# Rows of the band attention in another order: 3, 1, 4, 2, 5, 0, 6, 7 in place of 0 to 7

## The chip and the metric

The kernel runs on one core of a Trainium2 chip. The metric is the device time of one execution in microseconds, the median of three timed executions. The engines are PE (matmuls), DVE (vector work), ACT (activations), POOL (vector work on a second engine) and SP, whose queue here only issues DMAs.

## What is computed

One layer of a mixer on x of shape 1 x 1024 x 1024. One projection is cut into four head groups, each is gated, and an output projection and a layer norm follow. The change touches group B, a band attention with four heads of 64, in which a chunk of 64 positions sees itself and the eight chunks before it:

```python
def chunk_band_attention(q, k, v, rel_bias):
    ...
    s = jnp.einsum('bcqhd,bckhd->bchqk', qc, kb).astype(jnp.float32) * (dh ** -0.5)
    ...
    s = jnp.where(valid[None, :, None, None, :], s + bias[None, None], -jnp.inf)
    p = softmax_f32(s, v.dtype)
    o = jnp.einsum('bchqk,bckhd->bcqhd', p, vb)
    return o.reshape(bsz, seq, h * dh)

def hybrid_layer(x, mem, ...):
    proj = x @ w_in + b_in
    ...
    yb = chunk_band_attention(heads(bq), heads(bk), heads(bv), b_rel)
    yc = dsa_attention(heads(cq), heads(ck), heads(cv), ...)
    ...
    mixed = jnp.concatenate([ya * jax.nn.silu(a_g), yb * jax.nn.silu(bg),
                             yc * jax.nn.silu(cg), ym * jax.nn.silu(mg)], axis=-1)
    y = mixed @ w_out + b_out
    return layer_norm(DEEPNORM_ALPHA * x + y, ln_g, ln_b)
```

The queries of group B are taken in eight rows of 128. The rows do not depend on each other.

## The kernel before

The whole program is one core's stream of instructions, laid out by helpers that weave attention work with projection work. In the part that matters two stretches follow each other, one for each pair of heads of B. `mixes_of_b(pair)` makes eight items, one for each 128-query row `rb`. Row `rb` sees `n` keys: 128, 256, 384 and 512 for rows 0 to 3, and 640 for rows 4 to 7. `mix_of` gives an item its parts:

- `scores`: PE multiplies queries and keys (`qk` matmuls with 64 rows of weights, three products of high and low halves for each of two heads and each piece of up to 512 columns) into two `qk` banks for each piece. DVE reads them, adds the bias and writes the scores into a tile `sc`, one for each head, and keeps the maximum `mx`. ACT makes `nb` from it and takes the exponential in place. `turned` then lets POOL split the result into a high and a low half (`tensor_scalar`, L545, and `tensor_sub`, L546), and SP transposes both by DMA into a tile `pT`: one DMA for `n` up to 512 (L549), two for 640 (the high half at L551, the rest at L552).
- `values`: PE multiplies `pT` with the value tile in `pv_mm`, two matmuls for each 128 keys and head, into a bank `d["pv"]`, whose tag is "pv" for even rows and "pt" for odd rows. Behind the last, DVE and ACT normalise the row (`o`).
- `close`: PE transposes `o` (a `pt` matmul), DVE gates it (`mix`), and SP stores it.

`parts_behind(items, 2)` sets the order of the parts: at step t come the scores of item t, the first values of item t-2, the close of item t-3 and the other values of item t-2. `weave` goes through these parts and spreads 64 filler steps evenly between them, each of three projection matmuls (`acc`, 128 rows of weights, 512 columns): `weave(parts_behind(mixes_of_b(0), 2), B[1].all(B1_ORDER), RATES[2], pace(3), LAG_T)`, and then pair 1 with fillers from C. A third stream, the search for the top 256 keys of group C, is woven in by `pace`; its passes (`jk` on DVE, `jka` on ACT, and at the end a scan on DVE) fill both engines.

An engine takes its instructions in the order in which a scheduler puts them, so an instruction that waits holds up everything behind it on its engine. The tile `sc` has SB = 4 buffers and `pT` has TB = 4, two rows of two heads each; an item therefore uses the buffers of the item two places ahead of it, and its first score must wait until the transposes of that item have read `sc`. The weight loads for the projections (`raw`) stand on SP's queue among the transposes.

## Time and profile before

| | us |
|---|---|
| median of three runs (lowest, highest) | 674.93 (674.66, 675.70) |
| the profiled run | 675.66 |
| its span, first to last instruction | 673.9 |
| PE busy | 638.5 (95%) |
| DVE, ACT, POOL busy | 479.7, 427.0, 355.4 |
| pair 0, from its first `qk` to pair 1's | 315.79 to 390.70 |
| pair 1, to the first `qk` of group C | 390.70 to 461.97 |

The profile is of one execution. A busy PE in it is not PE at its peak: matmuls overlap, and the distance from the start of one to the start of the next says more than the length of one. The times of a pair are read between the first score matmuls of what follows, since the order of work is the same in both kernels ahead of 315.79 and behind 461.97 us.

### The profile page before, as it was taken

What the parts mean: (1) busy time and instruction counts of PE and PEld (TensorE: products, weight loads), DVE (VectorE), ACT (ScalarE), POOL (GpSimd) and SP (SyncE); (2) the same over time, 40 slices, a digit from 0 to 9 for tenths busy, and PEclk for the clock granted to TensorE, in tenths of its full rate; (3) what the DMA queues carried; (4) which work ended last, traced back from release to release, by engine and by line L of the source; (5) the groups of instructions that cost most, each with busy time, mean ns of one, the idle gap of its engine ahead of it and who ended that gap; (6) DMA issues with size and microseconds to landing.
All of it is one profiled execution on the core that took longest, in us unless ns stands there. A gap on an engine that the chain in (4) does not pass through costs nothing.

```text
span 673.9 us, 11068 instructions
## 1 busy us (share of the span) xinstructions
PE 638.5 (95%) x3698; PEld 484.8 (72%) x3698; DVE 479.7 (71%) x1165; ACT 427.0 (63%) x947; POOL 355.4 (53%) x354
## 2 busy tenths in 40 slices
PE   4889999999999999989899999999999999999995
PEld 3867777767877777767566776677677777778785
DVE  6584254688866898999788778985567559787535
ACT  4665244576799988785888986556456675356210
POOL 3682320306346697483547435993214776557851
PEclk9999999999999999999998999999999999999998
DMA  9783520102134545354439625744001574225111
GB/s 281 237 302 107 162 59 23 40 18 82 60 110 110 132 104 121 72 132 130 96 79 149 132 72 110 126 86 143 31 17 48 177 236 140 75 86 196 63 62 63
DMA packets 121669, 75.30 MB, mean 112 GB/s; under 512 B 58976, under 2 KB 111500, under 8 KB 121612
## 3 DMA queue, kind: packets, MB, share of 16 engines
q1 hardware_dynamic: 121612, 74.59, 41.4%
q8 instruction: 29, 0.48, 0.3%
q14 instruction: 28, 0.23, 0.1%
HBM read 46.44 MB, written 17.64 MB: 95 GB/s over the span
## 4 chain that ended last, share of the span: by engine, by line
PE 51%; DVE 12%; ACT 12%; POOL 10%; issue 7%; DMA 7%; SPq 0%; POOLq 0%; DVEq 0%; ACTq 0%
PE acc L94 36%; PE qk L94 6%; PE pv L94 5%; ACT jka L94 5%; DMA pT<-sc 3%; POOL wblk L208 3%; PE pt L94 3%; DVE jk L94 2%; POOL sc L546 2%; ACT sc L94 1%; DMA raw<-in_w_in 1%; DMA xt<-in_x 1%; DMA hr<-h_dram 1%; POOL rs L134 1%; ACT relu L94 1%
## 5 line engine op out<-in xcount | busy, mean ns | idle before, releaser
L94 PE MATMUL acc<-hTh,wblk 128*128 128x512 f32 (+1 forms) x960 | 316.8, 399 | 4.4 <-ACT vT L94 1.7
L94 PEld LDWEIGHTS acc<-hTh,wblk 128*128 128x128 f32 x960 | 176.8, 188 | 50.3 <-issue 6.7
L94 PE MATMUL acc<-hTl,wblk 128*128 128x512 f32 (+1 forms) x480 | 189.9, 396 | 0.0
L208 POOL TENSOR_TENSOR wblk<-raw,wblk 128x512 fp32r<-128x512 f32 x72 | 99.9, 1392 | 127.9 <-ACT wblk L94 124.8
L94 ACT ACTIVATE jka<-score,cand 128x768 int8<-128x768 f32 (+2 forms) x93 | 96.6, 1038 | 15.7 <-DVE cand L94 15.0
L94 PEld LDWEIGHTS acc<-hTl,wblk 128*128 128x128 f32 x480 | 90.5, 188 | 20.6 <-issue 4.0
L94 PEld LDWEIGHTS <-pT 128*128 128x128 f16 x656 | 46.6, 99 | 32.5 <-issue 18.9
L94 PE MATMUL pv<-v,pT 128*128 128x192 bf16 (+1 forms) x528 | 55.4, 238 | 5.6 <-DMA pT<-sc 5.1
L546 POOL TENSOR_TENSOR sc<-sc 128x512 f16<-128x512 f32 (+4 forms) x48 | 55.9, 1170 | 2.3
L94 ACT ACTIVATE wblk<-raw 128x512 fp32r<-128x512 f32 x72 | 44.6, 627 | 18.6 <-PE acc L94 9.1
L94 DVE SCALAR_TENSOR_TENSOR score<-relu,iw,score 128x384 f32<-128x384 f32 (+5 forms) x42 | 42.7, 1039 | 18.4 <-ACT relu L94 16.5
L94 PE MATMUL acc<-woh,mh 128*128 128x512 f32 (+1 forms) x144 | 55.3, 384 | 0.0
L94 PE MATMUL acc<-wol,mh 128*128 128x512 f32 (+1 forms) x144 | 53.6, 372 | 0.0
L94 PE MATMUL acc<-woh,ml 128*128 128x512 f32 (+1 forms) x144 | 53.5, 373 | 0.0
L545 POOL TENSOR_SCALAR sc<-sc 128x512 f16<-128x512 f32 (+4 forms) x48 | 33.4, 698 | 32.3 <-ACT sc L94 28.8
L94 ACT ACTIVATE relu<-qk 128x384 f32<-128x384 f32 (+2 forms) x80 | 35.5, 533 | 22.5 <-PE qk L94 22.4
L94 ACT ACTIVATE sc<-sc,nb 128x640 f32<-128x640 f32 (+7 forms) x64 | 46.5, 729 | 1.2
L94 ACT ACTIVATE pT<-pt 128x512 f16<-128x512 f32 (+3 forms) x48 | 22.4, 485 | 31.2 <-PE pt L94 30.8
L94 ACT ACTIVATE o<-o,ri 128x64 f32<-128x64 f32 x96 | 28.1, 341 | 17.4 <-DVE o L94 17.3
L94 DVE TENSOR_SCALAR_CACHE_REDUCE jk<-planes,lo 128x384 bf16<-128x384 uint16 (+2 forms) x48 | 35.6, 742 | 1.1
L94 DVE TENSOR_SCALAR_CACHE_REDUCE jk<-planes,cand 128x384 bf16<-128x384 bf16 (+2 forms) x45 | 33.5, 744 | 1.1
L94 DVE TENSOR_REDUCE o<-pv 128x128 f32<-128x384 f32 x48 | 26.4, 549 | 10.2 <-PE pv L94 10.0
(204 smaller groups left out, 1241.2 us busy)
## 6 DMA issues: line engine op xcount, KB each, us to landing
raw<-in_w_in SPq DMA_DIRECT2D x32, 512.0 KB, 3.8
xt<-in_x SPq DMA_DIRECT2D x8, 512.0 KB, 4.7
h_dram<-xt SPq DMA_DIRECT2D x8, 512.0 KB, 5.8
gate<-t SPq DMA_DIRECT2D x16, 256.0 KB, 2.1
rawo<-in_w_out SPq DMA_DIRECT2D x8, 512.0 KB, 3.9
hr<-h_dram SPq DMA_DIRECT2D x8, 512.0 KB, 4.9
out<-hr SPq DMA_DIRECT2D x7, 512.0 KB, 2.6
gate<-gate SPq DMA_DIRECT2D x48, 64.0 KB, 2.0
```

The source lines that it names most:

```text
L94: ins = op(*a, **k)
L134: G.tensor_scalar(tmp, var, EPS, 0.0, ALU.add, ALU.add)
L208: G.tensor_sub(t[:, 1], r, f32(t[:, 0]))
L545: G.tensor_scalar(high, sc[:, :n], 1.0, 0.0, ALU.mult, ALU.add)
L546: G.tensor_sub(rest, sc[:, :n], high)
```

## The change

The rows of B are taken in the order of a new table, `B_ITEMS`, in both pairs, and the bank of the values goes by the item's position (even or odd) instead of by its row number. `place` keeps its default of 0 for the other callers of `mix_of`. The number of instructions on each engine stays what it was.

```diff
--- before.py
+++ after.py
@@ -39,6 +39,7 @@
 
 C0_FIRST, LATE = (0, 1, 6, 7, 5), "17 16 15 14 04 13 03 12 02 11 10"
 HR = 2
+B_ITEMS = 3, 1, 4, 2, 5, 0, 6, 7
 BOOST_Q = 2000
 WH = (0, 0)
 MHB = 2
@@ -703,7 +704,7 @@
 
         return Item(scores, [], [lambda: values(0), lambda: values(1)], close)
 
-    def mix_of(kt, rb, kb0, st, near, far_of, last):
+    def mix_of(kt, rb, kb0, st, near, far_of, last, place=0):
 
         by_dma = kt < 4
         q, k, v3 = st
@@ -750,7 +751,7 @@
 
         def values(odd, c):
             if not odd and not c:
-                d["pv"] = bank(("pv", "pt")[rb % 2 and by_dma], "pv")
+                d["pv"] = bank(("pv", "pt")[place], "pv")
             ph, pl = [part[c:] for part in d["p", odd]] if by_dma else d["p", odd, c]
             for j in range(min(4, nk - c)):
                 pv_mm(d["pv"], odd, ph[j], pl[j], v3[:, kb0 + c + j, odd], c + j == 0, c + j == nk - 1)
@@ -1120,7 +1121,7 @@
 
     def mixes_of_b(pair):
         items = []
-        for rb in range(NB):
+        for i, rb in enumerate(B_ITEMS):
             kb0 = max(0, rb - 4)
             nfar = max(0, (rb + 1 - kb0) * P - 256)
 
@@ -1130,7 +1131,7 @@
                 store_mix(2 + pair, rb, t)
 
             items += mix_of(2 + pair, rb, kb0, B[pair].stacks(), lambda odd: nearB[pair][:, odd, :],
-                            lambda lo, hi, nfar=nfar: farB[:, 384 - nfar + lo:384 - nfar + hi], last)
+                            lambda lo, hi, nfar=nfar: farB[:, 384 - nfar + lo:384 - nfar + hi], last, i % 2)
         return items
 
     weave(parts_behind(mixes_of_b(0), 2), B[1].all(B1_ORDER), RATES[2], pace(3), LAG_T)
```

What moves is shown at three places, each a few rows of PE or DVE in the order in which the engine takes them. A number behind a name is a tile's; `acc` is a filler's matmul, `pT` a transposed tile, L94 and L95 are the same helper's line before and after.

PE in pair 0, where the first values start. Rows that only repeat are left out. Before, row 0's second head (`pT_3650`) and row 1's first (`pT_3701`):

```order
L94 MATMUL acc_3814<-hTl1_118,wblk_3657 128x512
L94 LDWEIGHTS pT_3650
L94 MATMUL pv_3745<-v3_3097,pT_3650 128x192
L94 MATMUL pv_3745<-v3_3097,pT_3650 128x128
L94 MATMUL acc_3814<-hTh1_117,wblk_3657 128x512
L94 MATMUL acc_3934<-hTh0_115,wblk_3926 128x512
L94 MATMUL acc_3934<-hTl0_116,wblk_3926 128x512
L94 MATMUL qk_3875<-kh_3489,qh_2871 128x384
L94 MATMUL acc_3934<-hTh0_115,wblk_3926 128x512 x2
L94 LDWEIGHTS pT_3701
L94 MATMUL pv_3818<-v3_3097,pT_3701 128x192
```

After, row 3's first head (`pT_3647`), scores of row 2 (`qk_3812`, `qk_3813`) and row 3's second head (`pT_3652`); each of its heads has four such pairs of matmuls, of which one stands here:

```order
L95 MATMUL acc_3960<-hTh0_115,wblk_3955 128x512 x2
L95 LDWEIGHTS pT_3647
L95 MATMUL pv_3757<-v3_3097,pT_3647 128x192
L95 MATMUL pv_3757<-v3_3097,pT_3647 128x128
L95 MATMUL qk_3812<-kh_3489,qh_2871 128x384
L95 MATMUL qk_3813<-kh_3489,qh_2871 128x384
L95 MATMUL qk_3812<-kh_3489,ql_2872 128x384
L95 LDWEIGHTS pT_3652
L95 MATMUL pv_3757<-v3_3097,pT_3652 128x192
L95 MATMUL pv_3757<-v3_3097,pT_3652 128x128
L95 MATMUL qk_3813<-kh_3489,ql_2872 128x384
```

The first values are row 3's, four pairs of matmuls for a head instead of one, and no filler stands between the heads.

DVE in pair 0, where an item first uses buffers that a transpose must have read. Before, row 3 (`sc_3785`) behind row 2 (`sc_3715`, `sc_3716`):

```order
L94 TENSOR_SCALAR jk_3588,c_1606<-planes_1519,lo_1608 128x640
L94 RECIPROCAL ri_3843<-rsum_3682 128x2
L94 ISA sc_3715,mx_3717<-qk_3718,farB_128 128x128
L94 ISA mx_3717 128x1
L94 ISA sc_3716,mx_3717<-qk_3719,farB_128 128x128
L94 ISA sc_3715,mx_3717<-qk_3718,nearB_3620,mx_3717 128x256
L94 ISA sc_3716,mx_3717<-qk_3719,nearB_3620,mx_3717 128x256
L94 ISA sc_3785,mx_3787<-qk_3788,farB_128 128x256
L94 TENSOR_TENSOR bit_1605<-c_1606,bar_1536 128x6
```

After, row 4 (`sc_3717`, `sc_3718`), whose buffers are row 3's:

```order
L95 TENSOR_SCALAR jk_3588,c_1606<-planes_1519,lo_1608 128x640
L95 RECIPROCAL ri_3780<-rsum_3626 128x2
L95 ISA sc_3717,mx_3719<-qk_3720,farB_128 128x384
L95 ISA mx_3719 128x1
L95 TENSOR_TENSOR bit_1605<-c_1606,bar_1536 128x6
L95 ISA sc_3717,mx_3719<-qk_3722,nearB_3620,mx_3719 128x256
L95 SCALAR_TENSOR_TENSOR thr_1603<-bit_1605,thr_1603 128x6
L95 SCALAR_TENSOR_TENSOR ql_3663<-acc_3838,bias_77,qh_3662 128x512
L95 TENSOR_SCALAR cand_1604<-thr_1603 128x6
L95 CAST lo_1608<-cand_1604 128x3
L95 TENSOR_SCALAR jk_3676,c_1606<-planes_1519,lo_1608 128x384
L95 ISA sc_3718,mx_3719<-qk_3721,farB_128 128x384
```

The third item's scores have search operations and a projection's `ql` between their heads and behind their first piece.

PE in pair 1, where the scores of row 5 are made. Before, the first of its two pieces (`qk_4898` and `qk_4899`, one tile for each head) among fillers (`acc_4964`):

```order
L94 MATMUL qk_4898<-kh_3932,qh_3660 128x384
L94 MATMUL acc_4964<-hTl1_118,wblk_4853 128x512
L94 MATMUL acc_4964<-hTh1_117,wblk_4853 128x512
L94 MATMUL acc_4964<-hTh1_117,wblk_4856 128x512
L94 MATMUL qk_4899<-kh_3932,qh_3660 128x384
L94 MATMUL qk_4898<-kh_3932,ql_3661 128x384
L94 MATMUL qk_4899<-kh_3932,ql_3661 128x384
L94 MATMUL qk_4898<-kl_3933,qh_3660 128x384
L94 MATMUL qk_4899<-kl_3933,qh_3660 128x384
L94 MATMUL acc_4964<-hTl1_118,wblk_4856 128x512
```

After, both pieces (`qk_4826` and `qk_4827`, `qk_4828` and `qk_4829`) behind the close of row 3 (`pt_4798`):

```order
L95 MATMUL pt_4798<-ident_66,o_4738 128x128
L95 MATMUL qk_4827<-kh_3958,qh_3662 128x384
L95 MATMUL qk_4826<-kh_3958,ql_3663 128x384
L95 MATMUL qk_4827<-kh_3958,ql_3663 128x384
L95 MATMUL qk_4826<-kl_3959,qh_3662 128x384
L95 MATMUL qk_4827<-kl_3959,qh_3662 128x384
L95 MATMUL qk_4828<-kh_3958,qh_3662 128x256
L95 MATMUL qk_4829<-kh_3958,qh_3662 128x256
L95 MATMUL qk_4828<-kh_3958,ql_3663 128x256
L95 MATMUL qk_4829<-kh_3958,ql_3663 128x256
L95 MATMUL qk_4828<-kl_3959,qh_3662 128x256
L95 MATMUL qk_4829<-kl_3959,qh_3662 128x256
```

Eleven of the twelve score matmuls of row 5 follow each other now; before, fillers stood between them at three places, of which the rows show the first two. Over the whole two stretches, the listing of before has fillers interrupted 32 times in pair 0 and 38 times in pair 1, that of after 27 and 25 times.

## Rows read from the trace of the kernel before

**Rows 1.** By stretch: length, busy (instructions) of PE, PEld, DVE, ACT, POOL, clock, DMA.

```profile
316.00:391.00 75.00, 69.72 (x398) 50.55 (x397) 62.11 (x204) 65.68 (x146) 40.61 (x44) 0.98 0.55 106
391.00:462.00 71.00, 69.56 (x402) 49.70 (x401) 58.84 (x154) 45.66 (x103) 50.82 (x45) 1.00 0.55 112
```

**Rows 2.** PE in time (start, length, operation): first scores of pair 0, pair 1, C.

```profile
315.79 0.32 PE L94 MATMUL qk<-kh,qh 64*128 64x128 f32 x1
...
390.70 0.32 PE L94 MATMUL qk<-kh,qh 64*128 64x128 f32 x1
...
461.97 0.33 PE L94 MATMUL qk<-kh,qh 64*128 64x128 f32 x2
```

**Rows 3.** PE in time, pair 0: waits, in brackets with what ended them.

```profile
336.37 0.31 PE L94 MATMUL pv<-v,pT 128*128 128x192 bf16 x2 [1.43 <-DMA pT<-sc]
...
358.82 0.26 PE L94 MATMUL pv<-v,pT 128*128 128x192 bf16 x1 [0.92 <-DMA pT<-sc]
...
360.79 0.33 PE L94 MATMUL pv<-v,pT 128*128 128x128 bf16 x2 [0.67 <-DMA pT<-sc]
```

**Rows 4.** Table by stretch: the low clock behind those waits.

```profile
361.00:364.40 3.40, 3.40 (x26) 2.94 (x23) 2.81 (x12) 2.89 (x8) 1.84 (x3) 0.50 0.67 128
```

**Rows 5.** PE in time: a score matmul between fillers, and scores in a group.

```profile
316.61 0.39 PE L94 MATMUL acc<-hTh,wblk 128*128 128x512 f32 x1
316.92 0.38 PE L94 MATMUL qk<-kh,qh 64*128 64x256 f32 x1
317.24 0.50 PE L94 MATMUL acc<-hTh,wblk 128*128 128x512 f32 x1
317.57 0.39 PE L94 MATMUL acc<-hTl,wblk 128*128 128x512 f32 x1
317.80 0.40 PE L94 MATMUL acc<-hTh,wblk 128*128 128x512 f32 x1
...
440.21 0.28 PE L94 MATMUL qk<-kh,ql 64*128 64x256 f32 x2
440.33 0.28 PE L94 MATMUL qk<-kl,qh 64*128 64x256 f32 x2
```

**Rows 6.** PE in time: two value matmuls between fillers.

```profile
455.83 0.31 PE L94 MATMUL pv<-v,pT 128*128 128x192 bf16 x2
455.95 0.48 PE L94 MATMUL acc<-hTh,wblk 128*128 128x512 f32 x1
456.27 0.40 PE L94 MATMUL acc<-hTl,wblk 128*128 128x512 f32 x1
```

**Rows 7.** DVE, ACT, POOL in time at pair 0's start; the transposes' landing, 318 to 392.

```profile
325.77 0.28 DVE L94 CUSTOM_DVE_ANT_0 sc<-qk,nearB 128x128 f32<-128x128 f32 x1
...
336.48 0.42 DVE L94 CUSTOM_DVE_ANT_0 sc<-qk,farB 128x256 f32<-128x256 f32 x1 [1.63 <-DMA pT<-sc]
...
339.87 0.71 ACT L94 ACTIVATE sc<-sc,nb 128x512 f32<-128x512 f32 x1
...
341.47 1.16 POOL L546 TENSOR_TENSOR sc<-sc 128x512 f16<-128x512 f32 x1
...
DMA to landing us min/median/max: 2.3/2.7/5.1
```

**Rows 8.** All engines in time: the fifth row of pair 1, scores to values.

```profile
419.90 0.48 DVE L94 CUSTOM_DVE_ANT_0 sc<-qk,nearB,mx 128x256 f32<-128x256 f32 x1
...
420.65 0.74 DVE L94 SCALAR_TENSOR_TENSOR ql<-acc,bias,qh 128x512 fp32r<-128x512 f32 x1
...
421.62 0.82 ACT L94 ACTIVATE sc<-sc,nb 128x640 f32<-128x640 f32 x1
...
426.28 3.13 POOL L546 TENSOR_TENSOR sc<-sc 128x640 f16<-128x640 f32 x1
...
429.44 1.21 SPq L552 DMA_TRANSPOSE pT<-sc  x1
...
432.89 0.23 PE L94 MATMUL pv<-v,pT 128*128 128x128 bf16 x1 [1.07 <-DMA pT<-sc]
```

## The prediction

> **What bounds the kernel now.** I read the table by stretch first. Before 315.79 us and after 461.97 us the order of work is the same in both kernels, so only the two pairs of band heads can change: pair 0 from 315.79 to 390.70 us (74.91 us) and pair 1 from there to 461.97 us (71.27 us) [rows 2]. In both, PE is busy 93 and 98% of the time, DVE 83% [rows 1], so the end of a pair is PE's work plus PE's waits. Second, the waits: PE idles 5.28 us in the first stretch and 1.44 us in the second [rows 1], and most of it is `pv` matmuls waiting for a transposed probability tile `pT` to land: 1.43, 0.92 and 0.67 us in pair 0 [rows 3] and 1.07 in pair 1 [rows 8]. Third, the clock: TensorE is granted 0.50, its 1.2 GHz level, from 361.0 to 364.4 us, right after the stretch in which PE waited twice for row 4's `pT`; PE was busy all of those 3.40 us, so the fall costs at most half of it, 1.7 us [rows 4]. Everything else of the two pairs is PE's own pace: 74.91 - 5.28 - 1.7 = 67.9 us and 71.27 - 1.44 = 69.8 us.
>
> **Part one: the pace of PE, and what an interruption costs.** PE fills the time between attention pieces with projection matmuls (`acc`), 192 in each pair. The listings of both kernels show how often that run is interrupted: 32 times in pair 0 and 38 in pair 1 before, 27 and 25 after. Of these, interruptions that hold score matmuls (`qk`) number 13 and 18 before, 12 and 14 after; the others (`pv`, and small transposes) 19 and 20 before, 15 and 11 after.
> The price of one with `qk`: from the `acc` at 316.61 to the one at 317.80 us, 1.19 us pass in which three `acc` start; their own pitch is 0.23 (317.57 to 317.80), so 0.50 is left for one `qk` of 256 columns, which inside a group takes 0.12 at most (440.21 to 440.33). The interruption itself costs 0.38 [rows 5]. The price of one without `qk`: two `pv` start at 455.83, the next `acc` at 455.95, and its follower comes 0.32 later instead of 0.23: 0.09 [rows 6].
> These two prices can be tested on the kernel before: pair 1 has five more interruptions with `qk` and one more without, which makes 5 x 0.38 + 0.09 = 2.0 us, and its pace is 69.8 - 67.9 = 1.9 us slower. So I trust them. Pair 0 then gains 0.38 + 4 x 0.09 = 0.74, pair 1 gains 4 x 0.38 + 9 x 0.09 = 2.33, together 3.07 us. The bounds are 1.9 (the five with `qk` alone) and 3.9 (a quarter more).
> The Trainium skill (TensorEngine Tiling (Array Packing), "Key Properties") says that changing the tiling mode drains TensorE. `qk` is 64-row work and `acc` and `pv` are 128-row work, so by that rule a `pv` between `acc` would cost nothing, and the sum would be the five alone, 1.9 us, with a time of 674.5 us. The 0.09 behind a `pv` speaks against taking the rule for the whole cost.
>
> **Part two: the start of pair 0.** Row 3 (512 keys) now comes first instead of row 0 (128). DVE starts its scores where row 0's started, at 325.77, and row 1's pieces stand between its heads, so row 3's scores, six pieces of at most 0.48 with these, are done by about 328.4. ACT runs a search pass and two exponentials of 0.71, POOL a `tensor_scalar` and a `tensor_sub` of 1.16 for each head (the second head's `tensor_sub` now stands behind row 1's two `tensor_scalar`), and a transpose lands 2.3 to 5.1 us after its issue, here about 3 [rows 7]: the two heads land at about 335.3 and 338.1. PE, which has more filler ahead of its first `pv`, arrives at about 335.3: no wait for the first head, 1.7 for the second, about 0.5 for row 1's. Row 4 uses row 3's `sc` and `pT` buffers, and its first score on DVE waits for row 3's transpose, as row 3's did for row 1's before, 1.63 us [rows 7]; here that stall is about 3 us, and the search operations behind it on DVE wait too. Row 4 then lands at about 348.4 and 350.9, PE comes at 347.1: waits of 1.3 and 1.3. The weight load that stood directly ahead of row 4's transposes on SP's queue stands ahead of row 5's now, where PE has slack of 1 us or more; row 5 to row 7: 0.2. Sum 5.0 against 5.28: -0.28. Each landing is an estimate good to 1.2 us, so the sum may be 3 to 8.
> The clock I leave as it is: PE is again kept waiting twice, one wait close behind the other, now near 348 us instead of 359. It can go to -1.7 (no fall) or +1.7 (a second one).
>
> **Part three: pair 1.** PE's only long wait before is for row 4, the fifth row, at 432.89 us (1.07 us). Its way: last score piece at 419.90, exponential of the second head at 421.62, `tensor_sub` on POOL at 426.28, which takes 3.13 us while DVE runs the search's scan, transpose at 429.44 [rows 8]. Now the fifth row is row 5, also 640 wide, and POOL's order around it is the same (sub, scalar, weight block, sub). Ahead of it DVE has scored rows 3, 1, 4, 2 instead of 0 to 3: one 640-wide row in place of a 128-wide one, two heads of 2 x 0.48 - 0.28 = 0.68, and a projection's low part `ql` of 0.74 (420.65) that stood behind [rows 7, 8]: 2.1 us later. It lands at 432.9 + 2.1 = 435.0, less what PE's gain in pair 0 passes on to DVE; I take 434.3. PE arrived at 431.8 before. Now ten more `acc` stand ahead of it (+2.3), seven interruptions fewer (4 x 0.38 + 3 x 0.09 = -1.8), four `pv` fewer (-0.3), and pair 0 ended 1.0 earlier: 431.0. The wait is 3.3 instead of 1.44 for the whole pair: +1.9, with bounds of 0 (POOL's `tensor_sub` misses the scan) and 5 (a weight load on SP delays the landing as well). Rows 6 and 7 stand 17 and 20 us behind it on PE and land in time. The changed bank of `pv` costs nothing: positions alternate between the same two banks as rows did.
>
> **Sum.** -3.07 - 0.28 + 1.9 = -1.45 against the profiled run of 675.66: 674.2. That run is 0.73 above the median of 674.93, so the forecast is 673.5 us. What can be told from no change is 0.2%, 1.35 us; the forecast lies just beyond it.
>
> **The rivals.**
> Rival A, faster: the clock does not fall, because PE's waits for row 4 (1.3 + 1.3 now, 0.92 + 0.67 before [rows 3]) come where it has been busy longer or are met by the landing. That takes 1.7 off: 671.8 us. For it: the mean clock of the first stretch, 0.98, leaves room for the one fall only [rows 1], so the wait of 1.43 at 336.37 brought none. Against: the new ones lie as close together as the old. Chance 0.18.
> Rival B, no change: PE gets ahead of a chain that does not get faster. The interruptions saved are in pair 1, 1.8 of them ahead of the wait for row 5, and every one saved there is waited for if the landing stands; and the landing may be a microsecond later. Then the 3.07 is spent: 674.9 us. For it: DVE is in order and full of search. Against: six interruptions and ten `acc` are saved behind the wait as well. Chance 0.24.
> Rival C, slower: one set of buffers carries rows 3, 4, 5 and 6, all the wide ones, so each wide row's first score stands behind the transposes of the one before. If row 3's second transpose lands one issue later (1.3 us) and row 5's in pair 1 meets the weight load (5.1 instead of 2.7 us to landing [rows 7]), DVE's stalls pass on to rows 4 and 5 and PE pays 1.3 + 2.4 on top of the waits above: 673.5 + 3.7 = 677.2 us. It decides when row 4's second head lands after 352 or row 5's in pair 1 after 437. For it: DVE stalled 1.63 behind a narrower row already. Against: the same buffers come round only every 18 us or so (two of eight rows of 75 us), and a wide row needs about 10 from its scores to the landing. Chance 0.25.
> The forecast itself, 672.3 to 674.7 with its own error: 0.33.
>
> **How the numbers follow.** Faster by over 0.2% (below 673.6): 0.20 of the forecast's 0.33, all of A, 0.05 of B: 0.43. Slower (above 676.3): 0.24 of C and 0.03 of B: 0.27. Same: 0.30. For 8 in 10 the range takes in A's centre and its better half by 0.8, and C's centre: 671.0 to 677.3 us.
>
> **What will show it.** The interruptions: pair 1 without its waits should take about 67.5 us, pair 0 without waits and clock about 67.2. The starts: `pv` waits for row 3's second head near 338 and for row 4's near 348 and 350 us, and one of about 3 us near 434. DVE should show a stall of about 3 us on `pT` near 332 to 335. The forecast is wrong if the waits of pair 0 pass 7 us, if that of pair 1 passes 5, or if the pace does not follow the count of interruptions.

## The result

| | median us (lowest, highest) | profiled run | its span |
|---|---|---|---|
| before | 674.79 (674.33, 675.70) | 675.66 | 673.9 |
| after | 682.75 (681.69, 683.67) | 683.67 | 681.9 |

The changed kernel is slower: ratio 1.0117, interval 1.0102 to 1.0131. The forecast was 673.5, the range 671.0 to 677.3. So the sign is wrong, and the time lies 5.4 us outside the range.

The table by stretch of the changed kernel, cut at the first score matmuls as [rows 2] were: length, busy (instructions) of PE, PEld, DVE, ACT, POOL, granted clock, share and GB/s of DMA. First pair 0 and pair 1, then the four places where the clock falls:

```profile
315.80:390.74 74.94, 70.41 (x398) 51.63 (x397) 59.38 (x193) 61.24 (x140) 40.46 (x44) 0.95 0.51 106
390.74:466.83 76.09, 70.04 (x401) 52.35 (x401) 64.91 (x165) 49.09 (x108) 47.64 (x45) 0.96 0.46 105
338.00:346.00 8.00, 6.64 (x29) 4.89 (x30) 7.20 (x30) 6.55 (x16) 2.39 (x3) 0.58 0.35 84
424.00:428.00 4.00, 3.19 (x12) 2.39 (x13) 3.91 (x17) 1.42 (x3) 1.28 (x1) 0.58 0.69 158
440.00:446.00 6.00, 4.73 (x19) 3.22 (x21) 4.72 (x11) 2.16 (x5) 1.75 (x3) 0.72 0.36 79
638.00:644.00 6.00, 5.19 (x17) 3.98 (x18) 4.79 (x9) 3.17 (x11) 5.40 (x5) 0.72 0.44 160
```

Pair 0 takes what it took (74.94 against 74.91 us [rows 2]), pair 1 takes 76.09 instead of 71.27, and what follows, the last part, whose order of work is unchanged, takes 681.9 - 466.83 = 215.07 instead of 211.93. Length less busy PE is PE's idle time: 4.53 us in pair 0 and 6.05 in pair 1, where [rows 1] gave 5.28 and 1.44.

A mean clock of 0.58 over 8 us is 0.42 / 0.50 x 8 = 6.7 us at the 1.2 GHz level, and half of that, 3.4, is the most it can cost. The falls of pair 1 are 3.4 us each at that level and cost at most 1.7 each. Before there was one such fall, of 3.4 us, in both pairs together [rows 4].

PE in time, the waits over 0.3 us in the two pairs (start, length, operation, and in brackets the wait and what ended it), which answer to [rows 3] and to the last of [rows 8]:

```profile
337.92 0.26 PE L95 MATMUL pv<-v,pT 128*128 128x192 bf16 x1 [1.19 <-DMA pT<-sc]
340.56 1.22 PE L95 MATMUL pv<-v,pT 128*128 128x192 bf16 x8 [1.36 <-DVE mx L95]
367.23 0.38 PE L95 MATMUL qk<-kh,qh 64*128 64x256 f32 x1 [1.06 <-DVE mx L95]
381.85 0.26 PE L95 MATMUL pv<-v,pT 128*128 128x192 bf16 x1 [0.91 <-DMA pT<-sc]
424.81 0.45 PE L95 MATMUL pt<-ident,o 128*128 128x128 f32 x1 [2.97 <-DVE mix L95]
437.71 0.30 PE L95 MATMUL pt<-ident,o 128*128 128x128 f32 x1 [0.76 <-DVE mix L95]
441.27 0.96 PE L95 MATMUL pv<-v,pT 128*128 128x128 bf16 x9 [2.32 <-DMA pT<-sc]
```

Two of them, 1.36 and 1.06 us, end when DVE has read a score bank. The kernel before has such a wait too, which the rows ahead of the prediction leave out:

```profile
353.63 0.44 PE L94 MATMUL qk<-kh,qh 64*128 64x384 f32 x1 [0.86 <-DVE mx L94]
```

The longest is of a kind that the prediction did not have: the `pt` matmul of a `close` waits at 424.81 for a `mix`. A `mix` is DVE's gating of the row closed before, and it reads that row's transpose out of a "pt" bank. There are three "pt" banks in turn, and the second head's score pieces and the values of odd positions also take them, so the close of the second row needs the bank that the gating of the first still holds.

Where was DVE? Its rows ahead of that gating (the search's end and a projection's `ql`; accumulator reads and the other rows between them left out):

```profile
415.19 0.62 DVE L95 SCALAR_TENSOR_TENSOR thr<-bit,thr 128x6 uint32<-128x6 uint32 x1
...
416.21 1.12 DVE L95 TENSOR_TENSOR thr<-thr,hi 128x3 uint32<-128x3 uint32 x1
...
419.01 1.35 DVE L95 SCALAR_TENSOR_TENSOR cand<-thr 128x3 f32<-128x3 f32 x1
420.40 1.01 DVE L95 TENSOR_SCALAR_CACHE_REDUCE jk<-score,cand 128x768 bf16<-128x768 f32 x1
...
421.45 1.15 DVE L95 TENSOR_SCALAR_CACHE_REDUCE jk<-score,cand 128x896 bf16<-128x896 f32 x1
...
422.52 0.75 DVE L95 SCALAR_TENSOR_TENSOR ql<-acc,bias,qh 128x512 fp32r<-128x512 f32 x1
423.19 1.27 DVE L95 TENSOR_SCALAR_CACHE_REDUCE jk<-score,cand 128x1024 bf16<-128x1024 f32 x1
...
424.38 0.28 DVE L95 TENSOR_TENSOR mix<-pt,gate 128x128 f32<-128x128 f32 x1
```

and the same in the kernel before:

```profile
412.09 0.15 DVE L94 SCALAR_TENSOR_TENSOR thr<-bit,thr 128x6 uint32<-128x6 uint32 x1
...
412.82 0.15 DVE L94 TENSOR_TENSOR thr<-thr,hi 128x3 uint32<-128x3 uint32 x1
...
413.49 0.62 DVE L94 SCALAR_TENSOR_TENSOR cand<-thr 128x3 f32<-128x3 f32 x1
414.14 1.01 DVE L94 TENSOR_SCALAR_CACHE_REDUCE jk<-score,cand 128x768 bf16<-128x768 f32 x1
...
415.08 0.28 DVE L94 TENSOR_TENSOR mix<-pt,gate 128x128 f32<-128x128 f32 x1
```

Before, the gating stands behind one of three counting passes and runs at 415.08; after, it stands behind all three and a `ql`, at 424.38, 4.8 us behind the transpose it reads (`pt` at 419.60). PE wanted the bank at 424.81 - 2.97 = 421.84. In a small way the wait was there before: PE stood still for the same gating, for one third of a microsecond.

```profile
415.42 0.38 PE L94 MATMUL qk<-kh,qh 64*128 64x256 f32 x1 [0.35 <-DVE mix L94]
```

The fifth row of pair 1, row 5 now (DVE's last score piece, POOL's second `tensor_sub`, the second head's transpose on SP's queue), answers to [rows 8]:

```profile
427.41 0.48 DVE L95 CUSTOM_DVE_ANT_0 sc<-qk,nearB,mx 128x256 f32<-128x256 f32 x1
```

```profile
436.38 2.26 POOL L547 TENSOR_TENSOR sc<-sc 128x640 f16<-128x640 f32 x1
```

```profile
438.66 1.20 SPq L553 DMA_TRANSPOSE pT<-sc  x1
```

Its scores are ready 7.5 us later than row 4's were (419.90), PE starts on its `pT` at 441.27 instead of 432.89, and waits 2.32 us for it. DVE's search had fallen behind on the way: a pass whose result (`bit`) DVE took at 381.62 us before was taken at 388.67 after. But most of these 7 us were made up again. The result of the search's last pass, before and after:

```profile
410.84 0.92 DVE L94 TENSOR_TENSOR bit<-c,bar 128x6 uint32<-128x6 f32 x1
```

```profile
414.31 0.16 DVE L95 TENSOR_TENSOR bit<-c,bar 128x6 uint32<-128x6 f32 x1
```

It ends at 411.76 before and at 414.47 after, 2.7 us later. So of the 9.3 us by which the gating is later, 2.7 are the search's lag. Another 3.6 lie between that result and the first counting pass (2.4 us before, 5.9 after), and 3.0 are the order: two more counting passes and a `ql` ahead of the gating.

### The profile page after: what moved, and what is told of

Read it like the earlier page. It is cut to its first block, busy times and chain, and to the rows that moved or that the text cites. A ratio compares the mean times of both kernels' runs of the same rounds, so it can differ in the third digit from the quotient of the medians.

```text
span 681.9 us, 11075 instructions
## 1 busy us (share of the span) xinstructions
PE 640.4 (94%) x3698; PEld 489.2 (72%) x3698; DVE 486.2 (71%) x1165; ACT 425.6 (62%) x947; POOL 351.6 (52%) x354
## 4 chain that ended last, share of the span: by engine, by line
PE 36%; DVE 5%; POOL 3%; DMA 3%; issue 3%; ACT 1%; SPq 0%; POOLq 0%; DVEq 0%; ACTq 0%
PE acc L95 25%; PE qk L95 4%; PE pv L95 4%; PE pt L95 2%; DMA pT<-sc 2%; DVE sc L95 1%; DMA hr<-h_dram 1%; POOL hr L1244 1%; DVE hr L95 1%; DVE jk L95 1%; POOL sc L546 1%; POOL hr L1243 1%; POOL sc L547 0%; DVE thr L95 0%; ACT jka L95 0%
## 5 line engine op out<-in xcount | busy, mean ns | idle before, releaser
L95 PE MATMUL acc<-hTh,wblk 128*128 128x512 f32 (+1 forms) x960 | 316.2, 401 | 4.4 <-ACT vT L95 1.7
L95 PEld LDWEIGHTS acc<-hTh,wblk 128*128 128x128 f32 x960 | 178.6, 190 | 51.5 <-issue 6.8
L95 PE MATMUL acc<-hTl,wblk 128*128 128x512 f32 (+1 forms) x480 | 190.8, 398 | 0.0
L95 ACT ACTIVATE jka<-score,cand 128x768 int8<-128x768 f32 (+2 forms) x93 | 96.5, 1038 | 21.7 <-DVE cand L95 20.9
L95 PEld LDWEIGHTS acc<-hTl,wblk 128*128 128x128 f32 x480 | 91.5, 191 | 20.8 <-issue 3.1
L95 PEld LDWEIGHTS <-pT 128*128 128x128 f16 x656 | 46.7, 99 | 32.0 <-issue 17.6
L95 PE MATMUL pv<-v,pT 128*128 128x192 bf16 (+1 forms) x528 | 53.5, 237 | 7.9 <-DMA pT<-sc 4.4
L547 POOL TENSOR_TENSOR sc<-sc 128x512 f16<-128x512 f32 (+4 forms) x48 | 58.5, 1228 | 1.8
L95 ACT ACTIVATE wblk<-raw 128x512 fp32r<-128x512 f32 x72 | 44.5, 627 | 20.6 <-PE acc L95 11.4
L546 POOL TENSOR_SCALAR sc<-sc 128x512 f16<-128x512 f32 (+4 forms) x48 | 30.4, 641 | 50.9 <-ACT sc L95 50.8
L95 DVE SCALAR_TENSOR_TENSOR score<-relu,iw,score 128x384 f32<-128x384 f32 (+5 forms) x42 | 42.8, 1040 | 18.4 <-ACT relu L95 16.4
L95 PE MATMUL acc<-woh,mh 128*128 128x512 f32 (+1 forms) x144 | 55.8, 388 | 0.0
L95 PE MATMUL acc<-woh,ml 128*128 128x512 f32 (+1 forms) x144 | 54.2, 378 | 0.0
L95 PE MATMUL acc<-wol,mh 128*128 128x512 f32 (+1 forms) x144 | 54.2, 376 | 0.0
L95 ACT ACTIVATE relu<-qk 128x384 f32<-128x384 f32 (+2 forms) x80 | 35.5, 532 | 22.5 <-PE qk L95 22.4
L95 ACT ACTIVATE sc<-sc,nb 128x640 f32<-128x640 f32 (+7 forms) x64 | 46.4, 728 | 0.8
L95 ACT ACTIVATE pT<-pt 128x512 f16<-128x512 f32 (+3 forms) x48 | 22.4, 485 | 31.1 <-PE pt L95 30.9
L95 DVE TENSOR_SCALAR_CACHE_REDUCE jk<-planes,lo 128x384 bf16<-128x384 uint16 (+2 forms) x48 | 35.7, 743 | 1.0
L95 ACT ACTIVATE o<-o,ri 128x64 f32<-128x64 f32 x96 | 27.9, 340 | 11.1 <-DVE o L95 10.9
L95 DVE TENSOR_REDUCE o<-pv 128x128 f32<-128x384 f32 x48 | 26.4, 549 | 11.4 <-PE pv L95 11.3
L95 DVE TENSOR_SCALAR_CACHE_REDUCE jk<-planes,cand 128x384 bf16<-128x384 bf16 (+2 forms) x45 | 33.5, 744 | 1.1
```

The source lines that it names most:

```text
L95: ins = op(*a, **k)
L546: G.tensor_scalar(high, sc[:, :n], 1.0, 0.0, ALU.mult, ALU.add)
L547: G.tensor_sub(rest, sc[:, :n], high)
```

## Experiments

In the tables, waits are length less busy PE. All ratios are against runs of the kernel before on the same chip; the intervals are 95%.

**The same two kernels again.** Both unchanged.

> The changed kernel once more, for its last part: there its profile loses 3.2 us in the output stage, whose instructions are in the same order in both kernels: a wait of 1.8 us on TensorE near 638 us and a fall of the clock behind it, after a load of hr from memory landed later. If that belongs to the change (the output stage reached 4.8 us later meets something at a fixed time), every profile of it shows the wait. If it is chance, this profile shows none, and the time is 680 us.

> The kernel before once more, for a second profile of it on this chip: how far its pairs, its waits and its last part differ from execution to execution. If the wait near 633 to 639 us in the output stage (0.66 to 1.81 us in every kernel with a new order so far) belongs to these kernels, it is absent here, as in the first profile; if it is chance, it may stand here too. Pair 0 74.9, pair 1 71.3, last part 211.9 us if nothing varies.

| | ratio (interval) | pair 0 | pair 1 | waits | last part |
|---|---|---|---|---|---|
| after | 1.0117 (1.0102, 1.0131) | 74.94 | 76.09 | 4.53 + 6.05 | 215.07 |
| after again | 1.0108 (1.0089, 1.0128) | 73.85 | 76.73 | 3.10 + 4.95 | 212.74 |
| before | 1 | 74.91 | 71.27 | 5.28 + 1.44 | 211.93 |
| before again | 0.9995 (0.9973, 1.0017) | 73.45 | 71.62 | 5.43 + 1.98 | 212.0 |

What comes back each time is pair 1: 76.1 and 76.7 against 71.3 and 71.6, with a wait of 2.97 and 2.89 for the gating. Pair 1 of the second profile:

```profile
391.23:467.96 76.73, 71.78 (x401) 53.48 (x400) 65.60 (x166) 50.15 (x111) 48.30 (x46) 0.93 0.46 104
```

Its waits are 1.1 us less than the first time and it still takes longer: a mean clock of 0.93 is some 10 us at the 1.2 GHz level, which can cost 5 us. The longer last part does not come back (212.74), so most of its 3.1 us was this one execution's; the second one lost 1.6 us to a clock fall near 52 us instead, far ahead of the change. In the kernel before, the clock fall near 361 did not come back.

**Each half alone.** The new order and the new bank rule in pair 0 only, and in pair 1 only:

```diff
-        for i, rb in enumerate(B_ITEMS):
+        for i, rb in enumerate(B_ITEMS if pair == 0 else range(NB)):
```

```diff
-        for i, rb in enumerate(B_ITEMS):
+        for i, rb in enumerate(B_ITEMS if pair == 1 else range(NB)):
```

> The new order in pair 0, the old one in pair 1. Theory 'lag': in pair 0 VectorE stalls for transposes (3.3 us at 335.5 and 2.2 us at 362.6 in the changed kernel), the search queued behind those stalls falls one pass, 5 to 7 us, behind and stays so, and pair 1 starts with VectorE late whatever its own order: pair 0 takes 74.9 us as in the changed kernel, pair 1 has TensorE waits of 3 to 6 us instead of 1.4 and one or two falls of the clock, 677 to 680 us in all. Rival 'own order': what pair 1 loses comes from its own rows in the order 3, 1, 4, 2; then this run has pair 0 at 74.9, pair 1 at 70 to 71.5 and 674 to 676 us.

> The old order in pair 0, the new one in pair 1. 'Lag': VectorE comes to pair 1 on time, its first score near 392 to 395 us instead of 397.8, the fifth row's scores end near 423 instead of 427.8, TensorE waits for it about 3 us, one fall of the clock: 674 to 677 us. 'Own order': TensorE waits 6 us and more in pair 1, two falls of the clock, 679 to 682 us.

| | ratio (interval) | pair 0 | pair 1 | waits | both pairs |
|---|---|---|---|---|---|
| pair 0 only | 1.0018 (0.9999, 1.0038) | 74.54 | 70.01 | 3.67 + 2.80 | 144.55 |
| pair 1 only | 1.0014 (0.9997, 1.0032) | 75.21 | 71.58 | 5.75 + 2.33 | 146.79 |

Neither half loses more than 0.2%, and neither interval excludes no loss at all: the pairs take 144.6 and 146.8 us against 146.2 before and 151.0 with both. (The 144.6 leave out nine `pv` of pair 1, which stand behind the first score matmul of C there; twelve `pv` in a group take 1.0 us before, so this is some 0.7 us.) With pair 0 only, 676.80 us lies between the two forecasts. So it is neither pair 1's own row order nor the lag that pair 0 hands on, each by itself. In both halves the gating of pair 1's first row runs earlier than after the whole change, at 417.5 and 419.9, and nobody waits long for it.

**Rows 2 and 4 exchanged.**

```diff
-B_ITEMS = 3, 1, 4, 2, 5, 0, 6, 7
+B_ITEMS = 3, 1, 2, 4, 5, 0, 6, 7
```

> The order 3, 1, 2, 4, 5, 0, 6, 7 in both pairs: rows 2 and 4 change places, so that row 4 uses the buffers of row 1 (256 keys) and the third item is 384 wide and not 640; fillers are interrupted 19 and 26 times (27 and 24 in the changed kernel by the same count, 32 and 37 before). If wide rows one behind the other in one set of buffers hold VectorE, this gives most of the loss back: VectorE's stall at the third item stays (it still waits for row 3) but the search is less late, TensorE waits under 5 us in all and no more than two falls of the clock, 671 to 676 us. If the loss is the late start of the first values (row 3 being first) or the mere presence of a wide row early, it stays at 679 to 683 us.

Ratio 1.0031 (1.0016, 1.0047); pairs 74.21 and 72.32 with waits of 5.67 and 3.57 us. The first gating of pair 1 runs at 418.57, behind two of the counting passes. Exchanging two neighbours moves the gating by 6 us and removes most of the loss; the time, 677.59 us, lies between the two ranges that I had set.

**Without the search in the pairs.** The search's passes are not woven into the two pairs but come later, in the kernel before and in the changed one. It then lies open elsewhere, so the total says nothing; the pairs do.

```diff
-PACE = ((10,), (8,), (9,), (10,), (15,))
+PACE = ((10,), (8,), (9,), (0,), (0,))
```

> The kernel before with no search woven into the two pairs (its paces there are 0; the search then runs behind pair 1, so the whole time is longer and only the two pairs are compared). Theory 'both together': the loss of the changed kernel needs the search being late on VectorE and the new order in pair 1. Without the search VectorE has slack: TensorE waits under 3 us in the two pairs here, pair 0 about 70 to 73 us and pair 1 about 69 to 70.

> The changed kernel, likewise without the search in the two pairs. 'Both together': the new order then loses nothing in pair 1, its fillers are interrupted less often, and its two pairs take as long as those of the kernel before without the search or up to 3 us less, with no wait of more than 2 us in pair 1. Rival: the wide rows in one set of buffers hold the chain by themselves, search or not: then this pair of kernels differs by 4 to 5 us as the originals do.

The changed kernel without it, pair 0 and pair 1:

```profile
314.94:386.19 71.25, 67.52 (x397) 49.85 (x396) 36.27 (x120) 39.53 (x96) 40.16 (x44) 1.00 0.51 111
386.19:453.71 67.52, 67.52 (x403) 49.55 (x402) 28.39 (x97) 35.37 (x85) 39.47 (x43) 1.00 0.55 118
```

The pairs take 138.77 us with the new order and 72.16 + 67.80 = 139.96 with the old one (totals 715.4 and 718.7). PE has no wait in pair 1 in either, and the new order loses nothing: the loss needs the search on DVE beside it. The 1.2 us that the order gains are no more than two profiles of one program differ by (146.18 and 145.07 for the kernel before).

**The new order with the old bank rule.**

```diff
-                            lambda lo, hi, nfar=nfar: farB[:, 384 - nfar + lo:384 - nfar + hi], last, i % 2)
+                            lambda lo, hi, nfar=nfar: farB[:, 384 - nfar + lo:384 - nfar + hi], last, rb % 2)
```

> The new order with the bank of the values by row number, as it was, instead of by position. Rows 3 and 1, 4 and 2, and 0 and 6 then follow each other in the same bank. If the second half of the change does what it is for, rows 1, 2 and 6 wait for the normalisation of the row ahead, about 1 us on TensorE for each of the three in each pair: up to 6 us slower than the changed kernel, 683 to 688 us. If the alternation costs nothing, 682 to 683 us as the changed kernel.

> The row order 3, 1, 4, 2, 5, 0, 6, 7 with the value banks by row number, once more and with more rounds, to see whether it is faster than the kernel before. By its first profile the pairs take 143.2 us against 146.2 before (and 145.1 and 144.9 in the two later looks at kernels with the old order), with two clock falls in it. Theory that the order of rows is worth its pace (interruptions 14 and 13 with scores, 7 and 4 without, against 13, 18, 19, 20) when no counting pass stands ahead of a gating: 0.996 to 0.999 of the kernel before, 672.5 to 674.5. Rival, that the clock falls take all of it in most executions: 0.999 to 1.002.

First 0.9978 (0.9955, 1.0002), then, with more runs, 0.9981 (0.9960, 1.0002). The pairs of the first:

```profile
316.18:387.44 71.26, 68.26 (x388) 51.47 (x388) 58.92 (x195) 62.04 (x141) 38.54 (x43) 0.98 0.50 102
387.44:459.40 71.96, 68.19 (x390) 51.42 (x390) 59.85 (x157) 45.63 (x102) 48.35 (x46) 0.98 0.51 115
```

The whole loss is gone. The 143.2 us for both pairs make the gain look larger than it is, since 19 `pv` of the last rows stand behind the first score matmul of C in this kernel, some 1.6 us; the medians have it at 0.2%, within their intervals. I had expected the old rule to leave the time as it was or to make it worse by putting neighbours into one bank. What happened is that the scheduler, given another bank for four of the eight rows of each pair (3, 2, 5 and 0), laid out everything else anew: interruptions 14 and 13 with `qk`, 7 and 4 without, and a search one pass further at most rows. The gating still comes late, at 423.01, but PE's next `pt` matmul stands at 423.43 and finds it done.

**Shorter counting passes.** The changed kernel with the three last counting passes of the search over 128 columns each instead of 768, 896 and 1024; so part of the counting is left out.

```diff
-            n = (RBS[i] + 1) * P
-            V.tensor_scalar(junk()[:, :n], score[RBS[i]], f32(cand[:, i:i + 1]), None, ALU.is_ge,
+            n = P
+            V.tensor_scalar(junk()[:, :n], score[RBS[i]][:, :n], f32(cand[:, i:i + 1]), None, ALU.is_ge,
```

> The changed kernel with one thing cut: the three counting passes of the search on DVE (768, 896 and 1024 columns, once in the program) look at 128 columns each, so part of the counting is left out. Row order, banks and the order of PE's work ahead of the passes stay. In the changed kernel the gating (mix) of pair 1's first row stood on DVE behind these passes, 1.01 + 1.15 + 1.27 us plus a projection's low part of 0.75, and PE waited 2.97 us for it at 424.81. Theory that this queue holds PE's next transpose: the wait falls by about the 2.5 us taken out, to under 0.8, the clock does not fall near 425, and pair 1 takes 71.5 to 73.5 us instead of 76.1; total 677.5 to 680.5. Rival, that the bank is held by something else (the values of an odd position, which share its ring): the wait stays over 2 us and pair 1 over 75 us, total 681 to 683. Rival, that the late search alone costs (PE then pays at row 5's landing instead): wait near 425 gone, but over 4 us at row 5's values, pair 1 over 75.

Ratio 1.0198 (1.0165, 1.0230); pairs 74.12 and 74.92. The wait did not fall to under 0.8 us; it stayed, which is what the rival on the bank had said. The rows, DVE and then PE:

```profile
424.18 1.15 DVE L95 TENSOR_SCALAR_CACHE_REDUCE jk<-score,vth 128x896 bf16<-128x896 f32 x1
...
425.25 0.29 DVE L95 TENSOR_TENSOR mix<-pt,gate 128x128 f32<-128x128 f32 x1
```

```profile
425.68 0.30 PE L95 MATMUL pt<-ident,o 128*128 128x128 f32 x1 [2.95 <-DVE mix L95]
```

The scheduler put the time into the next step of the search: a pass of the masks (`vth`) now stands ahead of the gating. So the edit did not isolate what it was meant to: the gating is late again, behind other work of the search, and PE's wait ends with it again. Whether it is the search ahead of the gating at all was left to the next experiment. (The last part, whose order changed as well, took 6.7 us more than after the change: score matmuls there waited up to 2.59 us for DVE, and the clock was at its 1.2 GHz level from 570.0 to 576.9.)

**The end of the search held back.** Every instruction stays. Five empty steps ahead of the three counting passes, with the pace raised to match, make the search's end come later. In the changed kernel and, as a control, in the kernel before:

```diff
-PACE = ((10,), (8,), (9,), (10,), (15,))
+PACE = ((10,), (8,), (9,), (10,), (20,))
...
+        for _ in range(5):
+            yield
         for i in range(NV, NR):
             n = (RBS[i] + 1) * P
             V.tensor_scalar(junk()[:, :n], score[RBS[i]], f32(cand[:, i:i + 1]), None, ALU.is_ge,
```

> The changed kernel, complete, with five empty steps in the search ahead of its three last counting passes, so that they come later. On DVE all is in the same order up to the two normalising operations of pair 1's first row, but then the gating (mix) of that row comes ahead of the counting passes instead of behind them. Theory that this queue on DVE holds PE's next transpose: the wait of 2.97 us near 425 is under 0.8 us, the clock does not fall there, pair 1 takes 71 to 73 us instead of 76.1 and 76.7; total 676.5 to 680. Rival, that the bank or the row order makes the wait: over 2 us again near 425, total 681 to 684. Rival, that PE pays the time at row 5's values instead: wait near 425 gone, over 4 us near 437 to 442, total 680 to 684.

> Control: the kernel before with the same five empty steps. There the gating of pair 1's first row stood between the counting passes and PE did not wait for it. Theory: nothing to gain, 0.998 to 1.003 of the kernel before, pair 1 71 to 72.5 us. Rival, that moving the end of the search later helps by itself: under 0.997.

The changed kernel with it, 676.91 us, ratio 1.0015 (0.9998, 1.0033). Pair 0 and pair 1; DVE at the gating; PE there:

```profile
317.41:391.52 74.11, 70.53 (x397) 51.83 (x396) 58.73 (x192) 60.40 (x137) 39.79 (x44) 0.95 0.51 107
391.52:464.12 72.60, 67.83 (x401) 50.28 (x401) 66.20 (x163) 47.77 (x108) 46.68 (x46) 1.00 0.55 110
```

```profile
421.70 0.73 DVE L95 SCALAR_TENSOR_TENSOR ql<-acc,bias,qh 128x512 fp32r<-128x512 f32 x1
422.35 0.28 DVE L95 TENSOR_TENSOR mix<-pt,gate 128x128 f32<-128x128 f32 x1
...
425.77 1.01 DVE L95 TENSOR_SCALAR_CACHE_REDUCE jk<-score,cand 128x768 bf16<-128x768 f32 x1
```

```profile
423.16 0.30 PE L95 MATMUL pt<-ident,o 128*128 128x128 f32 x1
...
427.71 0.59 PE L95 MATMUL pv<-v,pT 128*128 128x192 bf16 x6 [1.97 <-DMA pT<-sc]
```

The gating comes ahead of the passes, PE does not wait for it, and the clock stays at 1.00 through pair 1: 72.60 us instead of 76.09 and 76.73. This run decides on the search's place: by the ratios (1.0117 and 1.0108 without the hold) 6.3 to 6.9 of the 7.3 to 7.9 us are gone, and in the profiles 3.5 to 4.1 of them in pair 1. It speaks against the bank as the cause, since the bank rule is the changed kernel's. Of the idle time little went (6.05 and 4.95 to 4.77), since PE now waits 1.97 us for a transpose and, at 459.79, 1.33 for another. The gain is clock, the 3.4 us and more that the falls of pair 1 could cost, while the pace is 1.2 us worse. PE's order further on in pair 1 changed with the hold as well, so the gain is the hold's. That the one wait for the gating made the loss is not isolated by it.

The kernel before with it: 672.35 us, ratio 0.9972 (0.9953, 0.9991), the only version here that is faster than the kernel before by its interval:

```profile
315.82:389.42 73.60, 68.04 (x398) 49.18 (x397) 60.65 (x203) 65.22 (x145) 40.72 (x44) 1.00 0.56 108
389.42:458.80 69.38, 69.21 (x402) 49.53 (x402) 61.70 (x154) 45.05 (x103) 49.66 (x45) 1.00 0.54 115
```

I had expected nothing to gain there, and had overlooked PE's 0.35 us for the gating (0.45 in the second profile). Pair 1's idle time goes from 1.44 and 1.98 to 0.17 us, among it the wait for row 4 [rows 8]. So the hold gives 0.3% without the new order too, and not all that it gives the changed kernel belongs to the change. With the search's end held back the old order is the better one: 0.9972 against 1.0015, with intervals that do not meet.

**Other orders and the hold.** Banks by row with another order; two orders, one for each pair, without and with the hold; and banks by row with the hold:

```diff
-B_ITEMS = 3, 1, 4, 2, 5, 0, 6, 7
+B_ITEMS = 1, 7, 0, 4, 3, 5, 6, 2
```

```diff
-        for i, rb in enumerate(B_ITEMS):
+        for i, rb in enumerate(((3, 1, 2, 4, 5, 0, 6, 7),(0, 1, 2, 3, 4, 5, 6, 7))[pair]):
```

> Another order, 1, 7, 0, 4, 3, 5, 6, 2, with the banks by row number. The listing has 13 and 13 interruptions with scores and 11 and 7 without (before 13, 18, 19, 20), and the search on DVE is as far as in the kernel with the banks by row (29, 30, 31, 31 passes ahead of pair 1's first four rows, against 28, 29, 29, 30 in the changed kernel). Theory that pace follows interruptions and the rest follows how far the search is: pace of pairs together 137.7 - 6.0 x 0.38 x 5/6 (5 fewer with scores, 1.9) - 21 x 0.09 (1.9) = 133.9 us, waits and clock falls as in the kernel before (6.7 + 1.7): pairs 142 to 145, total 671 to 675. Rival, that a row order with a wide row 7 second and a narrow one last makes DVE and the landings late whatever the search does: pairs over 147, total over 677.

> Pair 0 in the order 3, 1, 2, 4, 5, 0, 6, 7 and pair 1 in the old order 0 to 7, banks by position. The listing has the search at 28, 28, 28, 29 passes ahead of pair 1's first four rows, a pass later than in the changed kernel (28, 29, 29, 30) and two later than before (29, 29, 29, 30 at the same places or later). Interruptions 10 and 17 with scores, 9 and 20 without. Theory that a late search costs only where wide rows come first in the next pair: pair 1 71 to 73 us, total 673 to 677. Rival, that lateness of the search alone costs: pair 1 over 74.5, total over 679.

> The new row order with banks by row number and the same five empty steps. No wait for a gating was there to remove. Theory: as without them, 0.996 to 1.000 of the kernel before, 672 to 674.5 us. Rival, that the end of the search behind the gating also spares this kernel's 1.97 us wait for row 5's transpose near 441 and the clock fall behind it: pair 1 under 70 us, 669 to 671.5 us.

> Pair 0 in the order 3, 1, 2, 4, 5, 0, 6, 7, pair 1 in the old order, with the same five empty steps. Without them there was no wait for a gating over 0.49 us. Theory: unchanged within 0.3%, 673 to 676 us, pair 1 70.5 to 72 us. Rival, that a later end of the search meets the scores of C: last part over 214 us, total over 676.5.

| | ratio (interval) | pair 0 | pair 1 | waits |
|---|---|---|---|---|
| order 1, 7, 0, 4, ... | 1.0109 (1.0076, 1.0142) | 71.62 | 73.39 | 3.64 + 3.20 |
| two orders | 0.9995 (0.9975, 1.0016) | 73.67 | 71.00 | 5.50 + 1.54 |
| banks by row, held | 1.0010 (0.9993, 1.0027) | 71.81 | 72.94 | 2.57 + 4.15 |
| two orders, held | 0.9991 (0.9977, 1.0005) | 74.68 | 70.61 | 5.87 + 1.39 |

The first took 145.0 us for the pairs, the upper end of what I had set, and 683.25 us in all instead of 671 to 675: it lost its 1.1% in the last part, which took 220.1 us. Its order there is another one too, score matmuls wait 1.69 and 1.72 us for DVE, and the clock is at its 1.2 GHz level from 562.5 to 569.3. Nor was its pace as counted: without waits and clock the pairs take 145.0 - 6.84 - 1.7 = 136.5 us, where the prices of the interruptions gave 133.9. Two orders has the search later than the changed kernel (28, 28, 28, 29 passes ahead of pair 1's first rows; the last pass's result at 417.4 us, against 414.5) and loses nothing: lateness alone does not cost. In the last two of the table the hold gained nothing; PE's waits for a gating were at most 0.5 us there without it.

## Why the prediction was wrong, point by point

The forecast for the profiled run was 674.2 us, and it took 683.67. By parts, the prediction has 73.9 us for pair 0, 70.8 for pair 1 and nothing for the rest. Pair 0 took 1.0 us more than that, pair 1 5.3, and the last part 3.1, which the second profile has at 0.8. In that profile pair 0 is as forecast and pair 1 takes 5.9 us more. So pair 1 carries the miss.

**The pace: right in kind, too small.** Without waits and clock, pair 0 took 74.94 - 4.53 - 3.4 = 67.0 us and pair 1 76.09 - 6.05 - 3.4 = 66.6, where the prediction said 67.2 and 67.5. The gain was 4.1 us rather than 3.07, a little beyond the bound of 3.9. The two prices were never tested apart from each other, and for the order 1, 7, 0, 4 they gave 2.6 us too much. One sum beside them is off: with 1.9 us for the pace the time comes to 675.66 - 1.9 - 0.28 + 1.9 - 0.73 = 674.65 us and not 674.5.

**The start of pair 0: right in sum, not in its parts.** 4.53 us of waiting against 5.0. DVE's stall behind row 3 came as forecast, 3.33 us at 335.49, and PE's wait for row 3's second head ended at 337.92 (forecast 338.1) and was 1.19 (forecast 1.7). But the two waits of 1.3 for row 4 did not come. In their place stand 1.36 at 340.56 and 1.06 at 367.23, both for score banks that DVE had not read: DVE's stalls passed straight on to PE, as rival C had it. That the sum came out is luck; in the second profile it was 3.10.

**The clock: wrong, a step that failed.** Its term was 0, bounded at 1.7 either way. It cost up to 3.4 - 1.7 = 1.7 us more in pair 0, which is that bound, and up to 3.4 in pair 1 (5 in the second profile), where I gave it no term although I forecast 3.3 us of waiting there. In both profiles of the changed kernel both long waits of pair 1 come with a fall. Nor is the fall of pair 0 a chance: every one of the eleven profiles with row 3 first in pair 0 and the search in place has one between 339 and 349 us, for 6.8 us in ten of them, next to waits of 0.95 to 2.25 us like the 1.19 and 1.36 above. None of the four profiles with the old order in pair 0 and the search has a fall there, and two of them have one near 361.

**Pair 1: the wait, the other step that failed.** "Ahead of it DVE has scored rows 3, 1, 4, 2 instead of 0 to 3 ... 2.1 us later" counts score pieces, and takes the search on the same engine to stand where it stood. It did not: row 5's scores were 7.5 us late. The search's last pass was 2.7 us behind, the small operations after it took 2.9 us more, and the three counting passes, formerly between the pieces of row 4's scores, now stood in one block ahead of row 5's. The same block held up the gating of the first row. The prediction followed the chain scores, exponential, transpose, and never asked which bank a `close` needs. The waits were 6.05 us instead of 3.3, beyond the bound of 5 (4.95 in the second profile). Together: pair 1 took 2.75 us more by its waits, up to 3.4 by the clock, and 0.9 less by its pace, which makes the 5.3 us; in the second profile 1.65, up to 5 and 0.9. By these bounds the clock can be as large a part as the waits.

Part of that block's length is not in its instructions. From `thr` at 415.19 to `cand`, six operations on at most 6 columns took 0.62 + 1.12 + 0.16 + 0.58 + 0.50 + 1.35 = 4.33 us; the same six before took 1.42. The long ones end when a POOL instruction ends:

```profile
415.08 0.73 POOL L546 TENSOR_SCALAR sc<-sc 128x640 f16<-128x640 f32 x1 [5.07 <-ACT sc L95]
415.90 1.42 POOL L547 TENSOR_TENSOR sc<-sc 128x640 f16<-128x640 f32 x1
...
418.93 1.41 POOL L547 TENSOR_TENSOR sc<-sc 128x640 f16<-128x640 f32 x1
```

415.08 + 0.73 = 415.81 is where DVE's 0.62 ends, 415.90 + 1.42 = 417.32 the end of its 1.12 (417.33), and 418.93 + 1.41 = 420.34 that of its 1.35 (420.36). The counting pass of 768 columns takes 1.01 with POOL busy and 1.01 before. The 2.9 us more of these six are as long as PE's wait, but no run removed them alone: the version with the hold has them too (4.31 us). That they make the wait is therefore argued, not shown. The Trainium skill (SBUF — State Buffer, "SBUF: two separate sides") says that DVE operations with two SBUF inputs, or in a two-port mode, share a port pair with GpSimd as an exclusive lock, and that whichever starts second is blocked for the whole instruction of the first; the three end times above agree to 0.02 us.

**The bank: wrong.** "The changed bank of `pv` costs nothing" was reasoned from the banks, and in the banks it may be so. But the rule is an input to the scheduler, and going back to the old one gave another order of work and took the loss away.

**The rivals.** C had the right sign and the mechanism in pair 0, but its price of 3.7 us, a late transpose of row 3 and a landing of 5.1 us for row 5, did not occur: row 5's second head landed 441.27 - 438.66 = 2.6 us after its issue. C's sign, row 5's landing after 437, did come, but because the scores were late and not by way of the weight load, and the time lies above C's 677.2 too. A's condition (no fall) was met only by other versions.

**What stays open.** Why the scheduler places the search's end so differently for neighbouring tables was not followed further; why DVE's search is 7 us behind at 381 to 388 us is only partly accounted for, by the stalls of 3.33 and 2.17 us. Why a wait brings a fall of the clock in one execution and not in another is open, and so is how much of the loss is the one wait for the gating, since no run removed it alone. How much of the first execution's longer last part belongs to the change is open as well.

## What to carry to other kernels

A change of order is a change of every queue. When a scheduler lays the program out, read for each engine what stands between an operation and the one that frees its buffer, low-priority filler above all, and compare that list before and after, not only the chain that was moved. Filler on an in-order engine is cheap until a small operation that another engine waits for (here a gating of 0.28 us) stands behind 3 or 4 us of it; then holding the filler back can be worth as much as a new order of the rows (0.9972 here, against 0.9978 and 0.9981). And count what the clock falls that come with waits can cost, not only the waits' length: in pair 1 that can be as much.

## What the runs showed of the hardware

The clock does not fall by a wait's length alone. The kernel before waited 0.92 and 0.67 us near 359 and 361 and fell to the 1.2 GHz level from 361.0 to 364.4 [rows 3, 4]; the same program, run again, waited 1.04 and 0.64 us at the same two matmuls, no less in sum, and kept 1.00 through the same stretch:

```profile
359.20 0.26 PE L94 MATMUL pv<-v,pT 128*128 128x192 bf16 x1 [1.04 <-DMA pT<-sc]
361.13 0.64 PE L94 MATMUL pv<-v,pT 128*128 128x128 bf16 x7 [0.64 <-DMA pT<-sc]
```

```profile
361.00:364.40 3.40, 3.27 (x29) 2.51 (x30) 3.06 (x15) 2.82 (x7) 1.99 (x2) 1.00 0.68 141
```

A wait of 1.97 us at 427.71 brought no fall in the changed kernel with the hold, and one of 1.97 us at 440.61 came with one in the second run of the banks by row, from 442.0 to 445.4. And near 52 us, where all the kernels do the same, a fall came in 4 of the 18 profiles and put the first `qk` of pair 0 up to 1.8 us later. So at these places a fall is a matter of chance, and one profile does not say how often it comes. At the start of pair 0 it is not: with row 3 first and the search in place it came in 11 of 11 profiles.

DVE's smallest operations are not always cheap: one on 3 columns took 0.15 us at 412.82 before, beside an idle POOL, and 1.12 at 416.21 after, beside a busy one. POOL's idle time in the kernel before, which reaches from 411.74 to 413.48:

```profile
413.48 1.32 POOL L545 TENSOR_SCALAR sc<-sc 128x512 f16<-128x512 f32 x2 [1.74 <-DVE thr L94]
```
